# Hybrid attention block on one core: a new account of a shared port in the planner, GpSimd kept out of the feed-forwards, a new order of the mixers

## The chip, the core and the metric

The kernel runs on one core of a Trainium2 chip. Five engines take part: TensorE (PE in the profile, its weight loads PEld) multiplies matrices, VectorE (DVE) and ScalarE (ACT) work element by element, GpSimd (POOL) does the same where both operands lie in SBUF, and SyncE (SP) issues the transfers from memory. Each engine serves its own queue in order and waits on semaphores for the others. The metric is the time of one execution in microseconds of the device; lower is better.

## The reference

Two layers of a diffusion transformer block over 512 latent tokens and 256 context tokens, 1024 wide, in float32. Per layer: modulation columns from a condition vector, a norm, one projection into the inputs of three mixers (neighbourhood attention, latent attention, a gated linear recurrence), the mixers, an output projection with a residual, a second norm, and a gated feed-forward of width 2816 with a residual.

```python
for l in range(DEPTH):
    sh_m, sc_m, g_m, sh_f, sc_f, g_f = _adaln(c, ada_w[l], ada_b[l])
    u = _modulate(_rmsnorm(h, norm_mix_g[l]), sh_m, sc_m) @ w_in[l]
    ...
    o_lat = jnp.concatenate([na_o, mla_o, lru_o], axis=-1)
    h = h + g_m * (o_lat @ w_out[l])
    h = h + g_f * _swiglu(_modulate(_rmsnorm(h, norm_ffn_g[l]), sh_f, sc_f),
                          ffn_w_gate[l], ffn_w_up[l], ffn_w_down[l])
    if not last:
        ...   # the same for the context tokens hc
return h
```

The last layer gives only the latent tokens, so its feed-forward has 512 columns, the first layer's 768.

## The kernel before

Tokens lie along the free dimension, channels along the partitions. Each float32 factor is split into a high part, rounded to the matmul's format, and the low rest (`split`, made of `copy` and `sub`, lines 544 to 554); a product is three matmuls (high x high, high x low, low x high). A weight tile lands in `wst`, its parts are `whi` and `wlo`; activations in pairs are `s`, other tiles `tmp`, `lo`, `hr`; `A` and `B` are accumulator tiles; `ast` and `acc` are weights and sums of modulation columns that are worked off as a fill beside other work.

The feed-forward (`ffn`, line 1441) uses a scheme with seven half-size products in place of eight. Its operands are made first, in `operands` (line 836): norms, sums and differences of column halves, and a split of each. The weights' sums and differences (`weights`, line 884) are made from two landed tiles: these are the instructions `wst<-wst,wst`. Then come 11 pairs of hidden tiles in six groups, each group ended by a part of the down projection (`deliver`, line 1376).

No instruction is issued as it is written. Every call records an operation with its cost on each engine that may run it: `"svg"` means ScalarE, VectorE or GpSimd, `"vg"` VectorE or GpSimd. `Order.place` (line 304) then runs through a model of the machine: for each engine it takes the operation that can start first (ties by rank), lets one with several engines run where the model ends it first, and keeps in `port` when VectorE and GpSimd hold a port to SBUF that the model takes them to share. An operation that would start while the other holds it starts when that ends:

```python
if e == "g" or e == "v" and op.both:
    a, b = port["v" if e == "g" else "g"]
    if a <= st < b:
        st = b
```

`both` marks operations with no operand in the accumulators. GpSimd has a handicap of 600 in `BIAS`. Each tag (`s6`, `wst`, ...) has a number of buffers; the model keeps the times at which they come free, and `Buf.tile` asks the tile pool for one of the tag, and the pool chooses the place. In a mixer the steps are recorded in the order of `PLAN`, with a shift of rank after each `@`. Roots (the power of -0.5 in `rstd`, line 674) run on GpSimd alone.

## Time and profile before

| | |
|---|---|
| three timed runs | 1825.57, 1832.43, 1832.73 us; median 1832.43 us |
| profiled execution | 1837.95 us, span 1835.4 us |
| TensorE busy | 1720.5 us (94%) |
| VectorE busy | 1340.2 us (73%) |
| ScalarE busy | 770.2 us (42%) |
| GpSimd busy | 407.5 us (22%) |
| first mixer, about | 50 to 503 us |
| first feed-forward, about | 503 to 1090 us, its operands to 560 |
| second mixer, about | 1090 to 1455 us |
| second feed-forward, about | 1455 to 1836 us, its operands to 1500 |

A row of a profile names line, engine, operation and the tiles out<-in without buffer numbers. Most lines are helpers: L518 is every matmul, L554 every operation with two tensors, L544 and L546 the copies and casts on ScalarE and VectorE, L588 a tensor with a scalar and a tensor, L697 the root. The time of a row is the engine's busy time, which includes what the engine spends held up inside an instruction; idle time stands apart, with what ended it.

### The profile page before, as it was taken

To read this page: it belongs to the slowest core of one execution; us is meant where nothing else is said; L and a number is where in the kernel's file an instruction comes from. 1 tells how busy PE (TensorE), PEld (TensorE's weight loads), DVE (VectorE), ACT (ScalarE), POOL (GpSimd) and SP (SyncE) were. 2 spreads that over 40 slices of the span, in tenths; PEclk is the share of its full clock that TensorE was granted. 3 is DMA by queue.
4 is the path that set the end of the run, shared out by engine and by line. 5 is a ranking of instruction groups with operands and counts; after the bars stand their busy time and mean duration, and the time that the engine had idled before them with its cause. 6 is when DMAs were issued, how large, how long until landed. Compare 5 with 4: busy or idle time off the path is not lost.

```text
span 1835.4 us, 27989 instructions
## 1 busy us (share of the span) xinstructions
PE 1720.5 (94%) x10616; PEld 1472.5 (80%) x10616; DVE 1340.2 (73%) x2361; ACT 770.2 (42%) x1382; POOL 407.5 (22%) x326
## 2 busy tenths in 40 slices
PE   8989999999979999999999989998889989999998
PEld 4877665767959898989899968776678788898897
DVE  6574356766498888877879677576686797788776
ACT  5282245664153343323223233744565343343343
POOL 0142133233072121210111022213243240001010
PEclk9999899999989999999999989999999989999999
DMA  8121123233012334243434141212011123323332
GB/s 336 58 74 62 39 69 104 78 116 127 29 35 90 105 98 129 81 141 112 151 125 138 61 142 47 65 58 72 24 38 30 35 65 108 104 93 98 98 104 92
DMA packets 90998, 166.66 MB, mean 91 GB/s; under 512 B 10480, under 2 KB 53872, under 8 KB 90864
## 3 DMA queue, kind: packets, MB, share of 16 engines
q1 hardware_dynamic: 90864, 164.88, 28.1%
q8 instruction: 83, 1.36, 0.3%
q14 instruction: 51, 0.42, 0.1%
HBM read 160.65 MB, written 4.19 MB: 90 GB/s over the span
## 4 chain that ended last, share of the span: by engine, by line
PE 64%; DVE 22%; DMA 5%; issue 4%; ACT 3%; POOL 2%; SPq 0%; DVEq 0%; ACTq 0%; POOLq 0%
PE A L518 36%; PE B L518 22%; DVE wlo L554 6%; PE B L524 5%; DVE tmp L554 3%; DMA ast<-in_ada_dram 3%; DVE s L554 3%; DVE wst L554 2%; DMA wst<-in_wg_dram 1%; DVE acc L588 1%; POOL rn L697 1%; DVE s L546 1%; DVE lo L588 1%; DVE lo L554 1%; DVE hr L588 1%
## 5 line engine op out<-in xcount | busy, mean ns | idle before, releaser
L518 PE MATMUL A<-s,whi 128*128 128x256 f32 (+2 forms) x2192 | 546.9, 341 | 17.6 <-ACT s L544 5.5
L518 PE MATMUL B<-s,whi 128*128 128x384 f32 (+2 forms) x2032 | 465.9, 323 | 17.8 <-ACT hr L544 4.3
L518 PEld LDWEIGHTS A<-s,whi 128*128 128x128 f32 x2192 | 375.5, 190 | 72.2 <-ACT s L544 7.4
L544 ACT CAST whi<-wst 128x1024 fp32r<-128x1024 f32 (+2 forms) x281 | 227.0, 817 | 439.9 <-PE A L518 225.8
L518 PEld LDWEIGHTS B<-s,whi 128*128 128x128 f32 x2032 | 347.6, 193 | 32.2 <-ACT hr L544 4.6
L518 PE MATMUL A<-s,wlo 128*128 128x256 f32 (+2 forms) x1064 | 345.7, 338 | 1.2 <-DVE wlo L554 1.2
L554 DVE TENSOR_TENSOR wlo<-wst,whi 128x1024 fp32r<-128x1024 f32 (+3 forms) x303 | 319.9, 1066 | 12.1 <-ACT whi L544 8.4
L518 PE MATMUL B<-s,wlo 128*128 128x384 f32 (+2 forms) x1016 | 301.9, 320 | 0.2 <-DVE wlo L554 0.2
L518 PE MATMUL A<-lo,whi 128*128 128x512 f32 (+1 forms) x776 | 216.7, 358 | 4.7 <-DVE hr L588 1.8
L518 PEld LDWEIGHTS A<-s,wlo 128*128 128x128 f32 x1064 | 197.4, 191 | 15.8 <-DVE wlo L554 2.0
L518 PEld LDWEIGHTS B<-s,wlo 128*128 128x128 f32 x1016 | 190.6, 193 | 3.4 <-DVE wlo L554 0.5
L697 POOL TENSOR_TENSOR rn<-rn,con 128x12 f32<-128x12 f32 (+5 forms) x44 | 84.6, 1925 | 445.0 <-DVE rn L561 437.8
L518 PEld LDWEIGHTS A<-lo,whi 128*128 128x128 f32 x776 | 136.6, 188 | 31.7 <-issue 3.3
L588 DVE SCALAR_TENSOR_TENSOR hr<-A,mod,hr 128x512 f32<-128x512 f32 (+1 forms) x153 | 100.6, 659 | 60.2 <-PE A L518 60.1
L554 POOL TENSOR_TENSOR wst<-wst,wst 128x512 f32<-128x512 f32 x35 | 54.3, 1553 | 371.2 <-DVE wst L554 328.1
L518 PE MATMUL A<-lo,wlo 128*128 128x512 f32 (+1 forms) x388 | 136.2, 356 | 0.0
L518 PE MATMUL A<-s,s 128*128 128x512 f32 (+1 forms) x508 | 120.5, 354 | 14.2 <-ACT lo L533 4.5
L518 PEld LDWEIGHTS A<-s,s 128*128 128x128 f32 x508 | 81.2, 194 | 36.5 <-ACT lo L533 10.1
L546 DVE CAST whi<-wst 128x1024 fp32r<-128x1024 f32 (+3 forms) x45 | 32.7, 727 | 101.1 <-PE A L518 82.0
L588 DVE SCALAR_TENSOR_TENSOR acc<-ast,cc,acc 128x256 f32<-128x256 f32 x168 | 88.5, 527 | 19.2 <-DMA ast<-in_ada_dram 17.8
L554 POOL TENSOR_TENSOR wlo<-wst,whi 128x512 fp32r<-128x512 f32 (+3 forms) x25 | 40.9, 1637 | 262.2 <-ACT whi L544 260.9
L518 PE MATMUL B<-s,s 128*64 128x256 f32 (+2 forms) x720 | 87.5, 347 | 0.7 <-DVE sm L1411 0.5
(206 smaller groups left out, 2371.4 us busy)
## 6 DMA issues: line engine op xcount, KB each, us to landing
ast<-in_ada_dram SPq DMA_DIRECT2D x320, 128.0 KB, 2.2
wst<-in_wg_dram SPq DMA_DIRECT2D x44, 512.0 KB, 3.5
wst<-in_wu_dram SPq DMA_DIRECT2D x44, 512.0 KB, 3.5
wst<-in_wd_dram SPq DMA_DIRECT2D x80, 256.0 KB, 2.7
wst<-in_win_dram SPq DMA_DIRECT2D x32, 512.0 KB, 3.7
wst<-in_wout_dram SPq DMA_DIRECT2D x16, 512.0 KB, 3.7
hr<-in_x_dram SPq DMA_DIRECT2D x16, 384.0 KB, 3.6
s<-in_ada_dram SPq DMA_DIRECT2D x8, 768.0 KB, 11.5
```

Of the source, the lines that this page charges most:

```text
L518: od.add({"t": c}, lambda e: nc.tensor.matmul(ap(out), lhsT=ap(lhsT), rhs=ap(rhs), start=start, stop=stop, skip_group_check=more), [out], ...
L524: od.add({"t": 109.0}, lambda e: nc.tensor.transpose(ap(out), ap(in_), ap(ident)), [out], [in_, ident])
L544: nc.scalar.copy(out=ap(out), in_=ap(in_))
L546: nc.vector.tensor_copy(ap(out), ap(in_))
L554: (nc.vector if e == "v" else nc.gpsimd).tensor_tensor(out=ap(out), in0=ap(a), in1=ap(b), op=op)
L588: lambda e: nc.vector.scalar_tensor_tensor(out=ap(out), in0=ap(a), scalar=ap(s), in1=ap(b), op0=op0, op1=op1),
L697: lambda e: nc.gpsimd.tensor_tensor(out=ap(r[:, :w]), in0=ap(r[:, :w]), in1=ap(C("mhalf", 0, w)), op=ALU.pow),
```

## The change

Four edits. **The port's model:** an operation is no longer put off while the other engine holds the port. It starts, and its cost grows by the time until the other is done; in the choice between engines the same time is added. **GpSimd in the feed-forwards:** with `od.alone` set, an operation that may run on several engines loses GpSimd. It is set in `operands` and in the loop over the hidden groups. What has GpSimd as its only engine (the roots) stays there. **Buffer places:** the model keeps the number of each free buffer beside its time, hands it to the tile as `slot`, and each place is a tag of its own with one buffer; the pool chooses no more. **The mixers:** both texts of `PLAN` are new, with other orders of steps and other shifts.

```diff
@@ -57,29 +57,29 @@
 PLAN, LEAD = [], {}
 for _text in ("""
-    latent_kv @-53, lru_out 1 @-1529, lru_in 0, lru_in 1 @20, near_v 1 @990, near_q 1, lru_gates 0 @695,
...
+    lru_start @133, lru_in 0, latent_kv @1410, near_v 1 @-2446, lru_in 1 @-141, lru_out 1, lru_gates 0 @-229,
...
@@ -115,14 +115,15 @@
 
     def tile(self):
         if self.real is None:
-            self.real = self.pool.tile(list(self.shape), self.dt, tag=self.tag, name=f"{self.tag}_{self.id}",
-                                       bufs=self.bufs)
+
+            tag = self.tag if self.bufs == 1 else f"{self.tag}_{self.slot}"
+            self.real = self.pool.tile(list(self.shape), self.dt, tag=tag, name=f"{self.tag}_{self.id}", bufs=1)
         return self.real
 
 
 class Tag:
     def __init__(self, bufs):
-        self.line, self.free, self.loose = [], [0.0] * bufs, 0
+        self.line, self.free, self.loose = [], [(0.0, i) for i in range(bufs)], 0
 
 
 class Ref:
@@ -240,7 +241,7 @@
 
     def __init__(self):
         self.ops, self.bufs, self.tags = [], [], {}
-        self.shift, self.lead, self.gate = 0, 0, None
+        self.shift, self.lead, self.gate, self.alone = 0, 0, None, False
 
     def add(self, cost, emit, writes, reads, table=None, heat=1.0, middle=False, shape=0, both=False):
 
@@ -248,6 +249,8 @@
 
         op = Op()
         op.heat, op.pe, op.middle, op.shape, op.both = heat, "t" in cost, middle, shape, both
+        if self.alone and len(cost) > 1:
+            cost = {e: c for e, c in cost.items() if e != "g"}
         op.i, op.emit, op.cost, op.table = len(self.ops), emit, cost, table
         op.rank = op.i + self.shift + self.lead
         deps = {}
@@ -349,13 +352,9 @@
                                        not b.loose and len(tg.free) <= j + 1):
                             blocked = True
                             break
-                        st = max(st, tg.free[j])
+                        st = max(st, tg.free[j][0])
                     if blocked:
                         continue
-                    if e == "g" or e == "v" and op.both:
-                        a, b = port["v" if e == "g" else "g"]
-                        if a <= st < b:
-                            st = b
                     if op.table is not None and e == "s" and table not in op.table:
                         st_key = st + 1300.0
                     elif e == "t" and op.shape != shape:
@@ -371,6 +370,10 @@
 
                     op = top[1]
                     fin_here = top[3] + op.cost[e] + BIAS[e]
+                    if e == "g" or e == "v" and op.both:
+                        a, b = port["v" if e == "g" else "g"]
+                        if a <= top[3] < b:
+                            fin_here += b - top[3]
                     other = min(max(clock[x], op.ready[x]) + op.cost[x] + BIAS[x] for x in op.cost)
                     fin_key = (top[0][0] + (0.0 if fin_here <= other + 1.0 else fin_here - other), op.rank)
                     top = (fin_key, op, e, top[3])
@@ -392,7 +395,7 @@
                     tg.loose += 1
                 else:
                     tg.line.remove(b)
-                tg.free.pop(0)
+                b.slot = tg.free.pop(0)[1]
             cost = op.cost[e]
             if e == "t":
                 if op.shape != shape:
@@ -400,6 +403,10 @@
                     cost += SWITCH
                 cost = clockgate.run(st, cost, op.heat)
             if e == "g" or e == "v" and op.both:
+
+                a, b = port["v" if e == "g" else "g"]
+                if a <= st < b:
+                    cost += b - st
                 port[e] = (st, st + cost)
             if e == "s" and op.table is not None and table not in op.table:
                 table = op.table[0]
@@ -417,7 +424,7 @@
                 if not b.users and not b.dram:
                     tg = self.tags[b.tag]
                     tg.loose -= b.loose
-                    tg.free.append(b.end)
+                    tg.free.append((b.end, b.slot))
                     tg.free.sort()
             for q in op.outs:
                 q.ndep -= 1
@@ -877,8 +884,10 @@
                 tt(right(4 + j), right(4 + j), right(j), ALU.subtract)
                 put(("T4", "T3"), j, pair(), 0, xs[4 + j][:, :n])
 
+        od.alone = True
         first()
         second()
+        od.alone = False
         return ops
 
     def weights(src, i):
@@ -1528,6 +1537,7 @@
             split(two[0][:, :H], two[1][:, :H], gate.u, "s")
             return [one, two]
 
+        od.alone = True
         for h0, hn in GROUPS:
             acts = []
             for i in range(h0, h0 + hn, 2):
@@ -1543,6 +1553,7 @@
             end = h0 + hn == HT
             stats = deliver(l, h, lambda ot: load_w(wd_d[l, ot, :, h0 * P : (h0 + hn) * P], hn * P, "s"), acts, 40, n,
                             parts(n) if end and l < DEPTH - 1 else None)
+        od.alone = False
         return stats
 
     units = [0]
```

What this does to the order, at three places. First GpSimd's queue at the start of the first feed-forward, before, from the two roots on (`rn`):

```order
L697 TENSOR_TENSOR rn_5098<-rn_5098,con_82 128x3
L697 TENSOR_TENSOR rn_5105<-rn_5105,con_82 128x3
L554 TENSOR_TENSOR wst_5062<-wst_4710,wst_5062 128x512
L554 TENSOR_TENSOR s_1114_5133<-lo_5114,s_1114_5133 128x384
L548 TENSOR_SCALAR s_1116_5154<-lo_5136 128x384
L554 TENSOR_TENSOR s_1115_5150<-lo_5125,s_1115_5150 128x384
L554 TENSOR_TENSOR s_1116_5154<-lo_5136,s_1116_5154 128x384
L548 TENSOR_SCALAR s_1115_5150<-lo_5168 128x384
L554 TENSOR_TENSOR s_1115_5150<-lo_5168,s_1115_5150 128x384
L548 TENSOR_SCALAR s_1117_5194<-lo_5142 128x384
L548 TENSOR_SCALAR s_1117_5194<-lo_5158 128x384
```

The same place now:

```order
L704 TENSOR_TENSOR rn_5098<-rn_5098,con_84 128x3
L704 TENSOR_TENSOR rn_5108<-rn_5108,con_84 128x3
L555 TENSOR_SCALAR whi_10437<-wst_10361 128x1024
L561 TENSOR_TENSOR wlo_10451<-wst_10313,whi_10425 128x1024
L561 TENSOR_TENSOR wlo_10467<-wst_10417,whi_10459 128x1024
L704 TENSOR_TENSOR rn_10493<-rn_10493,con_84 128x4
L704 TENSOR_TENSOR rn_10532<-rn_10532,con_84 128x2
```

After the two roots nothing of the feed-forward follows; the next row (`whi_10437`) belongs to the second layer's first weights, and the roots of that layer's norm stand behind a cast and two subtractions, as they do before.

VectorE's queue at the same start, before, in the last third of the operands:

```order
L554 TENSOR_TENSOR s_1124_5276<-tmp_5256,s_1124_5276 128x768
L554 TENSOR_TENSOR wlo_5309<-wst_5102,whi_5296 128x1024
L554 TENSOR_TENSOR s_1126_5306<-tmp_5281,s_1126_5306 128x768
L554 TENSOR_TENSOR lo_5168<-lo_5168,lo_5125 128x384
L546 COPY tmp_5337<-B_5200 128x384
L554 TENSOR_TENSOR wlo_5345<-wst_4770,whi_5322 128x1024
L554 TENSOR_TENSOR s_1128_5333<-lo_5158,s_1128_5333 128x768
L554 TENSOR_TENSOR wlo_5366<-wst_5062,whi_5351 128x1024
L554 TENSOR_TENSOR s_1130_5360<-hr_5178,s_1130_5360 128x768
L554 TENSOR_TENSOR wlo_5387<-wst_5254,whi_5376 128x1024
L554 TENSOR_TENSOR wst_5373<-wst_5373,wst_5254 128x512
```

And now:

```order
L561 TENSOR_TENSOR lo_5143<-lo_5143,lo_5110 128x384
L561 TENSOR_TENSOR lo_5154<-lo_5154,lo_5120 128x384
L561 TENSOR_TENSOR wlo_5320<-wst_5102,whi_5308 128x1024
L561 TENSOR_TENSOR lo_5171<-lo_5171,lo_5127 128x384
L561 TENSOR_TENSOR hr_5183<-hr_5183,lo_5137 128x384
L561 TENSOR_TENSOR s_1127_5317<-lo_5143,s_1127_5317 128x768
L561 TENSOR_TENSOR wlo_5350<-wst_4771,whi_5338 128x1024
L561 TENSOR_TENSOR wlo_5361<-wst_5059,whi_5346 128x1024
L561 TENSOR_TENSOR s_1128_5325<-lo_5154,s_1128_5325 128x768
L561 TENSOR_TENSOR s_1129_5356<-lo_5171,s_1129_5356 128x768
L561 TENSOR_TENSOR s_1130_5364<-hr_5183,s_1130_5364 128x768
```

The `lo`, `hr` and `s` instructions that were GpSimd's stand between the weights' subtractions: of eleven rows four are differences, four low halves and three the weights' work, where one was a difference, four were low halves, one a copy and five the weights' work.

TensorE's queue in the second mixer, at a step that transposes copies of a value tile (`pvt`), before, from the last matmuls of a job on:

```order
L518 MATMUL B_12878<-s_2472_12830,s_2252_11889 64x256
L518 MATMUL B_12878<-s_2481_12862,s_2252_11889 64x256
L524 MATMUL B_12966<-ident_65,pvt_12942 128x128 x2
L524 MATMUL B_12970<-ident_65,hr_11936 128x128 x2
L518 MATMUL A_12974<-s_2122_11239,s_2383_12563 128x512 x3
L518 MATMUL A_12974<-s_2122_11239,s_2383_12563 128x256 x3
L518 MATMUL A_12990<-s_2122_11239,s_2383_12563 128x512
```

And now, up to the transposes of the copy made at about the same place:

```order
L531 MATMUL B_12932<-ident_65,pvt_12097 128x128 x2
L525 MATMUL B_12929<-s_2473_12861,s_2247_11972 64x256
L525 MATMUL A_12942<-s_2115_11161,s_2383_12573 128x512
L531 MATMUL B_12948<-ident_65,hr_11340 128x128 x2
L525 MATMUL A_12942<-s_2115_11161,s_2383_12573 128x512 x2
L525 MATMUL A_12942<-s_2115_11161,s_2383_12573 128x256
L531 MATMUL B_12955<-ident_65,lo_12927 128x128
L531 MATMUL B_12957<-ident_65,pvt_12940 128x128 x2
```

Between the first transposes of a `pvt` and the next there are now matmuls of a score tile `A` and a transpose of another step; before, the transposes of `pvt_12942` and of the tile `hr_11936` follow the job's last matmul at once.

## Rows read from the trace of the kernel before

**Rows 1.** The page's head.
```profile
span 1835.4 us, 27989 instructions
```

**Rows 2.** By stage: length, busy (instructions) of PE, PEld, DVE, ACT, POOL, clock, DMA.
```profile
50.00:503.00 453.00, 430.29 (x2804) 334.65 (x2804) 266.85 (x534) 202.52 (x407) 125.28 (x97) 0.99 0.24 75
503.00:560.00 57.00, 40.55 (x198) 35.44 (x197) 52.18 (x75) 30.97 (x55) 36.84 (x27) 0.85 0.12 37
560.00:1090.00 530.00, 511.28 (x2915) 479.30 (x2914) 427.84 (x736) 173.19 (x276) 80.97 (x59) 1.00 0.37 115
1090.00:1455.00 365.00, 333.90 (x2108) 270.83 (x2108) 255.73 (x442) 183.63 (x340) 107.13 (x85) 0.95 0.16 50
1455.00:1500.00 45.00, 36.31 (x215) 33.40 (x214) 42.15 (x67) 24.58 (x48) 28.60 (x30) 0.77 0.15 48
1500.00:1836.00 336.00, 325.54 (x2170) 295.63 (x2168) 259.50 (x400) 130.54 (x215) 26.25 (x22) 1.00 0.31 98
```

**Rows 3.** TensorE's waits, 560 to 1090 us: who for whom, sum, times, longest.
```profile
PE B L518 <- DVE acc L588: 5.5, 5, 1.7
PE A L518 <- ACT s L544: 3.7, 4, 1.3
PE B L518 <- DVE tmp L554: 2.8, 3, 1.4
PE A L518 <- DVE tmp L554: 2.1, 4, 0.7
```

**Rows 4.** Timeline of VectorE, 538 to 555 us: start, duration, operation.
```profile
...
544.02 2.39 DVE L554 TENSOR_TENSOR wlo<-wst,whi 128x1024 fp32r<-128x1024 f32 x1
...
548.86 2.29 DVE L554 TENSOR_TENSOR wlo<-wst,whi 128x1024 fp32r<-128x1024 f32 x1
...
553.00 1.21 DVE L554 TENSOR_TENSOR wlo<-wst,whi 128x1024 fp32r<-128x1024 f32 x1
```

**Rows 5.** Timeline of GpSimd, the same stretch.
```profile
...
543.17 4.94 POOL L554 TENSOR_TENSOR s<-lo,s 128x768 fp32r<-128x768 f32 x2
548.08 1.98 POOL L554 TENSOR_TENSOR wst<-wst 128x512 f32<-128x512 f32 x1
550.14 2.12 POOL L554 TENSOR_TENSOR wst<-wst,wst 128x512 f32<-128x512 f32 x1
```

**Rows 6.** Groups of VectorE, 503 to 1090 us: busy us, mean ns, idle before.
```profile
L554 DVE TENSOR_TENSOR wlo<-wst,whi 128x1024 fp32r<-128x1024 f32 x64 | 89.1, 1408 | 0.8 <-ACT whi L544 0.5
L588 DVE SCALAR_TENSOR_TENSOR acc<-ast,cc,acc 128x256 f32<-128x256 f32 x168 | 88.5, 527 | 19.2 <-DMA ast<-in_ada_dram 17.8
...
L554 DVE TENSOR_TENSOR wst<-wst,wst 128x512 f32<-128x512 f32 x40 | 34.3, 861 | 0.1
```

**Rows 7.** Groups of VectorE, 803 to 835 us, in which GpSimd runs nothing.
```profile
L588 DVE SCALAR_TENSOR_TENSOR acc<-ast,cc,acc 128x256 f32<-128x256 f32 x8 | 3.8, 479 | 0.1
L554 DVE TENSOR_TENSOR wlo<-wst,whi 128x512 fp32r<-128x512 f32 x5 | 3.4, 682 | 0.0
...
L554 DVE TENSOR_TENSOR wlo<-wst,whi 128x1024 fp32r<-128x1024 f32 x2 | 2.5, 1225 | 0.0
L554 DVE TENSOR_TENSOR wst<-wst,wst 128x512 f32<-128x512 f32 x3 | 2.0, 685 | 0.0
L554 DVE TENSOR_TENSOR lo<-tmp,lo 128x768 fp32r<-128x768 f32 x1 | 0.9, 946 | 0.0
...
L554 DVE TENSOR_TENSOR tmp<-tmp,tmp 128x384 f32<-128x384 f32 x1 | 0.5, 547 | 0.0
```

**Rows 8.** Groups of GpSimd, 503 to 1090 us.
```profile
L554 POOL TENSOR_TENSOR wst<-wst,wst 128x512 f32<-128x512 f32 x23 | 38.5, 1676 | 231.8 <-DVE wst L554 200.3 <-DVE wlo L554 16.5 <-DMA ast<-in_ada_dram 14.8
L554 POOL TENSOR_TENSOR wlo<-wst,whi 128x512 fp32r<-128x512 f32 x12 | 17.6, 1466 | 83.5 <-ACT whi L544 83.5
```

**Rows 9.** TensorE's waits, 1090 to 1455 us.
```profile
PE B L524 <- POOL rn L697: 6.8, 2, 6.2
PE B L524 <- DVE pvt L546: 5.2, 4, 3.1
```

More of the change, by code (lines that the diff above doesn't have):

```diff
@@ new lines @@
+    latent_query 3 @56, latent_job 0 0 @523, near_bias 0, latent_put 1 @497, latent_job 1 2 @465,
+    latent_query 4 @-1072, latent_job 1 0 @442, latent_query 5 @-990, latent_job 1 1, near_job 0 1 @38,
+    latent_put 2 @61, out_part 1 @64, near_job 0 0 @-1, near_ctx 0 @-2037, latent_job 2 0 @-6, near_prep 2 @460,
+    near_bias 2 @-49, out_part 3 @-1893, latent_job 2 2 @-44, out_part 0 @-98, latent_job 2 1 @-896,
+    near_prep 1 @-11, near_job 2 0 @-53, near_job 2 1 @1, out_part 2 @109, near_ctx 1 @-50, near_bias 1 @821,
@@ new lines @@
+    near_ctx 2 @-7, near_job 1 0 @-20, out_part 4 @-974, near_job 1 1 @87, out_part 6 @-5, out_part 5 @361,
+    out_part 7
+""", """
+    latent_kv @-2, lru_in 0 @-45, lru_in 1 @110, lru_gates 0 @72, near_k 2 @-239, near_k 0, latent_k 0 @-2500,
+    lru_out 1 @462, lru_gates 1 @218, near_v 0 @2202, latent_rope @507, lru_out 0 @-158, latent_keys @-283,
+    latent_put 0, latent_q @806, latent_k 1 @-10, near_q 0 @-744, near_k 1 @-113, lru_start @-305, lru_scan 0 @768,
+    near_q 1, latent_query 1, near_q 2, latent_query 0 @-6, latent_k 2 @26, latent_v, near_v 2 @-305, near_v 1 @217,
+    near_prep 1 @-38, lru_scan 1 @56, latent_query 2 @1619, latent_job 0 0 @-131, latent_job 0 1 @1455,
+    latent_put 1 @14, latent_query 3 @82, latent_job 1 0 @191, latent_query 4 @38, latent_query 5 @68,
+    latent_job 1 1, latent_put 2, near_bias 1 @1199, latent_job 2 1 @2500, near_job 1 1 @-477, out_part 1,
+    near_job 1 0 @-700, near_prep 0 @-587, latent_job 2 0 @27, near_prep 2 @55, near_bias 0 @-103,
+    near_job 0 0 @2382, near_job 0 1, near_bias 2 @1121, out_part 0 @196, near_job 2 1 @-284, out_part 3 @21,
+    near_job 2 0 @-28, out_part 4 @1524, out_part 5 @301, out_part 7, out_part 6 @-990, out_part 2 @403
```

25 lines of the change are left out of this document (4 added, 21 removed).

## Prediction

> **What bounds the kernel now.** I read the head of the page first, then the busy times by stage, then who waits for whom on TensorE in the stages that stand out, and last single instructions where two engines meet. The profiled execution has a span of 1835.4 us [rows 1] and took 1837.95 us in all; the three timed runs have their median at 1832.43 us, 5.5 us below it. I make the sum against 1837.95 and take the 5.5 us off at the end.
>
> The table by stage [rows 2] has two stretches for each layer besides its mixer: the start of a feed-forward, in which its operands are made (503 to 560 and 1455 to 1500), and its body (560 to 1090 and 1500 to 1836). TensorE is the bound almost everywhere, and its idle time says what can be had at all: 453 - 430.3 = 22.7 us in the first mixer, 365 - 333.9 = 31.1 us in the second; 57 - 40.6 = 16.4 us and 45 - 36.3 = 8.7 us in the two starts; 530 - 511.3 = 18.7 us and 336 - 325.5 = 10.5 us in the bodies. That is 108 us; the first 50 us of the program hold the rest. In the starts VectorE is the engine that others wait for: 52.2 of 57 us and 42.2 of 45 us busy, TensorE's granted clock down to 0.85 and 0.77 on average. In the bodies VectorE is 81% and 77% busy, and where TensorE waits in the first one, it waits mostly for VectorE: 5.5, 2.8 and 2.1 us are the largest such sums, beside 3.7 us for ScalarE [rows 3].
>
> What GpSimd does in these stretches is seen from single instructions. Between 538.64 and 554.14 us VectorE never idles, yet the same subtraction of a 128x1024 tile takes 2.39 and 2.29 us and then 1.21 us [rows 4]. The first two lie beside GpSimd instructions with two tiles in SBUF; the last one begins at 553.00, after GpSimd's last one ended at 550.14 + 2.12 = 552.26 [rows 5]. So two engines at work here largely take turns.
>
> **The change, part by part.**
>
> *GpSimd out of the feed-forwards.* In the order, GpSimd's instructions between the roots ahead of the first feed-forward and the second mixer go from 84 to 5: a cast and two subtractions of the next mixer's weights and the two roots of its norm stay. In the second feed-forward they go from 49 to 1. VectorE gets 61 and 43 instructions more, ScalarE 21 and 6.
>
> First the start of the first one. In the 15.5 us from 538.64 VectorE runs nine instructions. At the durations of a stretch in which GpSimd is idle [rows 7] they come to 4 x 1.23 + 3 x 0.95 + 2 x 0.55 = 8.9 us. The six GpSimd instructions beside them, four of which stand in [rows 5], are two of 384 columns, two of 768 and two of 512: on VectorE 2 x 0.55 + 2 x 0.95 + 2 x 0.69 = 4.4 us. In one queue that is 13.3 us for 15.5, a gain of 2.2 us. In the rest of the stretch GpSimd's small casts go to ScalarE, which has room (31.0 of 57 us busy [rows 2]); I add nothing for it. The second start has tiles two thirds as wide and less GpSimd time (28.6 against 36.8 us): I take 1 us. Both ends: the two stretches' whole idle time on TensorE, 25 us, as a gain; as a loss, that VectorE takes the moved work and none of its long durations shrink. The moved additions and subtractions of the first start are some 11.5 us at the durations of rows 7, those of the second about 10; VectorE has 4.8 and 2.9 us left there, so 14 us are lost. I take -3 us, near the stretch that I could work out.
>
> Then the bodies. Taken together with the starts, three kinds of VectorE instruction show what the shared access costs: (1408 - 1225) x 64 = 11.7 us, (527 - 479) x 168 = 8.1 us and (861 - 685) x 40 = 7.0 us, 26.8 us in all [rows 6, 7]; kinds that I do not list add to it. Against it stand the moved ones: 24 + 12 of the two kinds of 128x512 in [rows 8], some three more of that size, 39 x 0.685 = 26.7 us, and about 22 others at up to 0.95 us, some 14 us: 41 us. So VectorE's total stays about where it is. What changes is when a result comes: a sum of two weight halves takes 0.69 us in place of 1.68, a low half 0.68 in place of 1.47 [rows 7, 8]. 23 x 0.99 + 12 x 0.78 = 32 us of delay go out of the chain that feeds the casts and, behind them, TensorE. Little of it is on the path: TensorE waits 18.7 us in all, and what it waits longest for is the accumulator of the modulation columns, whose instructions are among those slowed (527 for 479 ns). The three sums for VectorE in rows 3 are 10.4 us; I take a half of them, 5 us, and 2 of the second body's 10.5 us, where GpSimd has a third of the first body's time. Ends: -20 us (most of 18.7 and a bit of 10.5), and +10 us, if the fills' accumulators come later because VectorE now does GpSimd's part of them as well: what is queued behind a late accumulator on TensorE is the whole feed-forward, since a queue is served in order. I take -7 us.
>
> *The port's model and the mixers' new order.* Both change only who comes when. GpSimd keeps its share there (111 to 115 instructions in the first mixer with the program's head, 85 to 86 in the second), so its turns with VectorE stay, and no stage gets work or loses it. What can go are waits such as the 6.8 us for two roots and the 5.2 us for four copies ahead of transposes in the second mixer [rows 9]. The longest of each has a fate in the order: the root that TensorE waits 6.2 us for stands in the order behind the same three GpSimd instructions as before (a cast and two subtractions of 128x1024), so that wait stays; the copy that cost 3.1 us now has TensorE work of another kind between it and its transposes. Of the mixers' 53.8 us idle I take a tenth, -5 us. Ends: -25 us, about half of it; +20 us, if the new places suit the model and not the chip: twelve waits like the copy's 3.1 us less what went would do.
>
> *Buffer places set by the order.* Taken alone this leaves each engine's rows as they are, and only which earlier tile a few instructions wait for differs (288 of some 3,150 tiles get another predecessor, about as many a later one as an earlier one). Zero, with the waits for buffers hidden by TensorE's queue; the ends are a few us to either side, within those above.
>
> Sum: -3 - 7 - 5 = -15 us, 1837.95 - 15 = 1823 in a profiled execution, and 5.5 less as a median of runs: **1817 us**, 0.8% faster.
>
> A rule speaks against the change. The Trainium skill, "Perfetto Trace Analysis", section "Optimizing Scalar/DVE Operations", says that where DVE is saturated, handing work to Scalar or even GPSIMD may make sense, and adds that between GPSIMD and DVE it might not help since they share a read port. By the first half of it the starts, where VectorE is the saturated engine, would lose by taking work back; by the second half they would not. Rows 4 and 5 side with the second half here; the first half is what the slower rival below rests on.
>
> **The rivals.**
>
> *Slower: the starts become VectorE's.* One mechanism: GpSimd did some 21 us of VectorE's work in the two starts beside it, and taking turns was only part of it. For it speaks that VectorE is over 90% busy there and that its chain ends in TensorE's first products; against it that rows 4 show nearly every instruction stretched. It decides if the stretching gives back less than 21 - 7.7 = 14 us. If it gives nothing, +14 us and no gain in the bodies: 1832 + 14 = 1846 us. Chance 0.18, in which I count a mixer order that suits the chip less.
>
> *No change.* TensorE streams at its rate in the bodies, the delays that go were covered by its queue, and the mixers trade one wait for another; for it speaks that each wait in rows 3 and 9 is a few us, against it that a stretch like that of rows 4 has nothing to hide it. Gain 0 to 8 us, 1828 us. Chance 0.21.
>
> *Much faster: the mixers close up.* The new order takes out half of their 53.8 us of idle time, -25, with -10 from the feed-forwards: 1797 us. For it: a model that charges the port to the instruction that meets it is closer to rows 4; against it: the longest single wait of the second mixer stays. Chance 0.11.
>
> **How the numbers follow.** Forecast 0.50, slower 0.18, no change 0.21, much faster 0.11. I call 0.5% (9 us) what a measurement tells from no change. Of the forecast's case, -6 to -28 us, four fifths lie beyond 9 us: 0.40, and with the much faster case 0.51 plus a little of the others: faster 0.54, same 0.27, slower 0.19. The forecast's own range is 1804 to 1826 us. The range for 8 in 10 reaches into the cases at both sides: 1796 to 1843 us.
>
> **What would show it.** GpSimd's busy time falls by about 160 us to some 250 us, while VectorE's stays within 20 us of 1340. The subtraction of 128x1024 in the feed-forwards has a mean near 1.23 us in place of 1.41, the accumulation near 0.48. The first start gets shorter by 2 us or more and ends with TensorE's clock up no later. The 6.2 us wait for a root at the second mixer's start is still there. I am wrong if VectorE's busy time grows by the whole 64 us that it takes over, if the starts get longer, or if the mixers' lengths (453 and 365 us) move by more than 10 us either way.

## The result and the profile after

The changed kernel takes **1777.99 us** (median of four runs, 1776.80 to 1778.68) against 1831.5 us of the kernel before beside it: 0.9713 of its time, 95% interval 0.9691 to 0.9736. The forecast of 1817 us had the direction; the gain is 53.5 us, not 15, and the time lies below the range of 1796 to 1843 us.

The page's head of the changed kernel, to be read beside [rows 1] (before: GpSimd 407.5 us, VectorE 1340.2 us in 2361 instructions):
```profile
span 1776.7 us, 27829 instructions
PE 1698.7 (96%) x10616; PEld 1458.1 (82%) x10616; DVE 1308.9 (74%) x2452; ACT 783.5 (44%) x1413; POOL 248.6 (14%) x204
```
VectorE runs 91 instructions more in 31 us less.

For comparing stages I cut both traces at the same instructions: the first that makes a feed-forward's operands, the first that takes a product out of PSUM, the first of the next norm. "Start" is where a feed-forward's operands are made, "body" the rest of it. Before, first mixer to second body:
```profile
27.70:513.00 485.30, 458.11 (x2976) 354.20 (x2975) 296.43 (x605) 217.58 (x432) 127.65 (x100) 0.99 0.26 83
513.00:557.60 44.60, 30.15 (x125) 26.54 (x126) 42.53 (x55) 25.33 (x47) 32.79 (x24) 0.82 0.11 36
557.60:1096.40 538.80, 514.79 (x2933) 482.41 (x2931) 436.25 (x747) 176.37 (x281) 87.10 (x61) 0.99 0.37 114
1096.40:1456.90 360.50, 333.57 (x2107) 270.44 (x2107) 251.09 (x436) 182.63 (x338) 103.85 (x85) 0.96 0.15 49
1456.90:1487.10 30.20, 22.74 (x122) 20.27 (x121) 30.15 (x43) 17.75 (x36) 26.12 (x28) 0.74 0.17 53
1487.10:1832.50 345.40, 338.34 (x2257) 308.43 (x2257) 270.10 (x420) 137.11 (x226) 27.55 (x23) 0.99 0.31 96
```
And the changed kernel (columns of [rows 2]):
```profile
27.60:503.20 475.60, 455.62 (x2974) 353.31 (x2975) 294.21 (x600) 219.52 (x430) 131.38 (x105) 0.99 0.26 85
503.20:539.00 35.80, 28.48 (x115) 23.27 (x115) 35.76 (x68) 26.91 (x51) 0.00 (x0) 0.78 0.13 43
539.00:1059.10 520.10, 509.37 (x2946) 481.44 (x2947) 425.32 (x796) 184.68 (x297) 8.93 (x4) 0.99 0.38 120
1059.10:1413.80 354.70, 330.30 (x2107) 266.84 (x2106) 248.71 (x430) 181.88 (x343) 105.25 (x87) 0.98 0.15 48
1413.80:1443.80 30.00, 25.71 (x146) 22.57 (x146) 30.00 (x65) 21.72 (x45) 0.60 (x1) 0.77 0.16 53
1443.80:1773.80 330.00, 326.16 (x2232) 300.39 (x2232) 261.50 (x440) 135.23 (x224) 0.00 (x0) 0.99 0.31 100
```
The feed-forwards give 43 us (8.8 and 18.7 us in the first one's start and body, 0.2 and 15.4 in the second's), the mixers 15.5 us (9.7 and 5.8). The two profiled executions are 59.3 us apart (1837.95 and 1778.68), 6 more than the medians; most of that excess lies in the second body (next section). In the bodies VectorE has 49 and 20 instructions more and is busy 10.9 and 8.6 us less.

VectorE's groups from 503.2 to 1059.1 us, beside [rows 6]:
```profile
L595 DVE SCALAR_TENSOR_TENSOR acc<-ast,cc,acc 128x256 f32<-128x256 f32 x168 | 80.7, 482 | 19.7 <-DMA ast<-in_ada_dram 17.7 <-ACT acc L582 0.4
L561 DVE TENSOR_TENSOR wlo<-wst,whi 128x1024 fp32r<-128x1024 f32 x65 | 78.3, 1222 | 1.3 <-PE A L525 0.4 <-ACT whi L551 0.4
L561 DVE TENSOR_TENSOR wst<-wst,wst 128x512 f32<-128x512 f32 x63 | 42.0, 686 | 0.1
```
1408, 527 and 861 ns are now 1222, 482 and 686, within 3 ns the undisturbed durations of [rows 7]. On TensorE, 539 to 1059.1 us, beside [rows 3]: the wait for accumulators is 1.2 us in place of 5.5, and the largest sum belongs to the next norm, at the stage's end.
```profile
PE B L525 <- DVE tmp L561: 4.7, 3, 4.2
PE B L531 <- POOL rn L704: 3.3, 1, 3.3
PE B L525 <- DVE acc L595: 1.2, 2, 0.8
```

### The profile page after: what moved, and what is told of

Same layout as the page of the kernel before. It is cut to its first block, busy times and chain, and to the rows that moved or that the text cites. A ratio compares the mean times of both kernels' runs of the same rounds, so it can differ in the third digit from the quotient of the medians.

```text
span 1776.7 us, 27829 instructions
## 1 busy us (share of the span) xinstructions
PE 1698.7 (96%) x10616; PEld 1458.1 (82%) x10616; DVE 1308.9 (74%) x2452; ACT 783.5 (44%) x1413; POOL 248.6 (14%) x204
## 4 chain that ended last, share of the span: by engine, by line
PE 79%; DVE 9%; DMA 2%; ACT 2%; issue 1%; POOL 1%; SPq 0%; ACTq 0%; DVEq 0%; POOLq 0%
PE A L525 43%; PE B L525 31%; PE B L531 5%; DMA ast<-in_ada_dram 2%; DVE s L561 2%; DVE wlo L561 1%; DVE tmp L561 1%; DVE lo L595 1%; DVE s L553 1%; POOL rn L704 0%; ACT lo L540 0%; DVE acc L595 0%; DVE sm L614 0%; DVE wst L561 0%; DVE hr L595 0%
## 5 line engine op out<-in xcount | busy, mean ns | idle before, releaser
L525 PE MATMUL A<-s,whi 128*128 128x256 f32 (+2 forms) x2192 | 540.7, 338 | 10.6 <-DVE whi L553 2.0
L525 PE MATMUL B<-s,whi 128*128 128x384 f32 (+2 forms) x2032 | 456.7, 319 | 11.0 <-DVE tmp L561 3.7
L551 ACT CAST whi<-wst 128x1024 fp32r<-128x1024 f32 (+3 forms) x289 | 235.8, 827 | 415.0 <-PE A L525 228.0
L525 PEld LDWEIGHTS B<-s,whi 128*128 128x128 f32 x2032 | 341.4, 191 | 25.6 <-DVE s L561 6.7
L561 DVE TENSOR_TENSOR wlo<-wst,whi 128x1024 fp32r<-128x1024 f32 (+4 forms) x322 | 311.2, 976 | 14.0 <-ACT whi L551 9.6
L525 PE MATMUL A<-s,s 128*128 128x256 f32 (+1 forms) x508 | 119.2, 353 | 15.3 <-ACT lo L540 4.8
L595 DVE SCALAR_TENSOR_TENSOR acc<-ast,cc,acc 128x256 f32<-128x256 f32 x168 | 80.7, 482 | 19.7 <-DMA ast<-in_ada_dram 17.7
L561 DVE TENSOR_TENSOR wst<-wst,wst 128x512 f32<-128x512 f32 x132 | 87.8, 690 | 0.5
L555 POOL TENSOR_SCALAR whi<-wst 128x1024 fp32r<-128x1024 f32 x6 | 7.9, 1319 | 572.9 <-PE B L525 548.4
L551 ACT COPY s<-B 128x384 f32<-128x384 f32 (+2 forms) x143 | 63.8, 476 | 39.7 <-PE B L531 35.0
```

The costliest lines, as they stand in the source:

```text
L525: od.add({"t": c}, lambda e: nc.tensor.matmul(ap(out), lhsT=ap(lhsT), rhs=ap(rhs), start=start, stop=stop, skip_group_check=more), [out], ...
L551: nc.scalar.copy(out=ap(out), in_=ap(in_))
L555: nc.gpsimd.tensor_scalar(out=ap(out), in0=ap(in_), scalar1=1.0, scalar2=1.0, op0=ALU.mult, op1=ALU.mult)
L561: (nc.vector if e == "v" else nc.gpsimd).tensor_tensor(out=ap(out), in0=ap(a), in1=ap(b), op=op)
L595: lambda e: nc.vector.scalar_tensor_tensor(out=ap(out), in0=ap(a), scalar=ap(s), in1=ap(b), op0=op0, op1=op1),
```

## The experiments

Stage lengths below are between the same marks, in us, of one profiled execution (the edits follow); times are medians, ratios are to the kernel before run beside it, with 95% intervals. Stages in order: first mixer, start, body; second mixer, start, body.

| kernel | time, ratio | M1 | S1 | B1 | M2 | S2 | B2 |
|---|---|---|---|---|---|---|---|
| before | 1831.5 | 485 | 44.5 | 539 | 360.5 | 30.1 | 345 |
| changed | 1778.0, 0.9713 | 476 | 35.8 | 520 | 354.7 | 30.0 | 330 |
| a_alone | 1795.7, 0.9808 (0.9788-0.9828) | 480 | 36.5 | 519 | 355.5 | 30.7 | 334 |
| a_port | 1865.4, 1.0184 (1.0166-1.0203) | 506 | 43.2 | 540 | 373.9 | 30.0 | 341 |
| slots | 1832.6, 0.9995 (0.9980-1.0011) | 487 | 43.2 | 540 | 360.4 | 30.1 | 341 |
| a_plan2 | 1833.2, 1.0000 (0.9979-1.0022) | 488 | 40.6 | 538 | 364.6 | 30.2 | 340 |
| u_alone | 1819.8, 0.9924 (0.9901-0.9946) | 479 | 44.9 | 541 | 352.5 | 32.6 | 338 |
| u_plan | 1828.6, 0.9974 (0.9958-0.9990) | 507 | 36.8 | 517 | 370.7 | 30.7 | 332 |
| u_port | 1798.7, 0.9814 (0.9786-0.9842) | 486 | 36.8 | 518 | 362.2 | 30.4 | 331 |
| o_body | 1806.1, 0.9850 (0.9821-0.9878) | 486 | 45.2 | 520 | 357.8 | 33.5 | 333 |
| o_operands | 1827.5, 0.9970 (0.9950-0.9989) | 487 | 34.8 | 544 | 356.5 | 24.9 | 347 |
| t_late | 1780.5, 0.9705 (0.9678-0.9732) | 479 | 36.8 | 518 | 352.7 | 31.1 | 331 |
| t_beside | 1801.1, 0.9811 (0.9783-0.9840) | 477 | 35.8 | 522 | 355.0 | 31.4 | 346 |
| t_beside4 | 1825.2, 0.9960 (0.9945-0.9975) | 478 | 36.5 | 533 | 354.6 | 31.4 | 360 |
| w_on | 1800.0, 0.9815 (0.9790-0.9840) | 477 | 35.0 | 531 | 357.2 | 30.1 | 336 |
| f_on | 1796.4, 0.9806 (0.9787-0.9825) | 477 | 35.8 | 527 | 357.3 | 30.7 | 335 |
| x_all | 1884.6, 1.0272 (1.0244-1.0300) | 569 | 35.8 | 515 | 369.3 | 30.1 | 333 |
| b_bound | 1788.6, 0.9754 (0.9730-0.9778) | 479 | 35.8 | 515 | 363.5 | 30.7 | 331 |
| b_loads | 1800.5, 0.9826 (0.9801-0.9850) | 479 | 35.8 | 515 | 379.8 | 29.8 | 330 |

Before's B2 is 345 us in this one profile and 340 to 341 in three others that leave the body as it was, so some 5 of the 15.4 us belong to that execution. Stage lengths of single executions can be off by that much: a_alone's profile (1787.45 us) is its fastest run, 8 us under its median.

**One part done alone.** a_alone: the kernel before with
```diff
+        od.alone = True
         first()
         second()
+        od.alone = False
...
+        od.alone = True
         for h0, hn in GROUPS:
...
+        od.alone = False
```


> The kernel before with one part of the change: GpSimd takes no work in the feed-forwards (neither in the start nor in the body); table of the order, port model and buffer places as before. Theory A (most of the 54 us is GpSimd leaving the feed-forwards: VectorE's instructions no longer stretched beside it, and results earlier): 35 to 45 us faster than before, 1787 to 1797 us, with the two feed-forwards 30 us or more shorter and the mixers within 4 us. Theory B (most is the new table and port model, which fit each other): 5 to 15 us faster, 1817 to 1827 us. Prediction's slower rival (the starts become VectorE's): over 1832 us.

It is 38 us faster, as theory A has it, and the feed-forwards are 38 us shorter. The mixers are 5 us shorter each, where theory A allowed 4; that is in the one fast execution.

a_port: the kernel before with the new port model's lines only.
```diff
-                    if e == "g" or e == "v" and op.both:
-                        a, b = port["v" if e == "g" else "g"]
-                        if a <= st < b:
-                            st = b
...
+                a, b = port["v" if e == "g" else "g"]
+                if a <= st < b:
+                    cost += b - st
```


> The kernel before with one part of the change: only the new port model (an instruction that meets the other engine's starts at once and is charged the rest of its turn); GpSimd keeps its work in the feed-forwards. Theory A: within 9 us of before, 1823 to 1841 us. Theory B: 15 to 25 us faster, 1807 to 1817 us, mixers and feed-forwards alike.

Both theories missed: it is 32 us slower, all of it in the mixers (20.6 and 13.4 us).

slots: the kernel before with
```diff
+            tag = self.tag if self.bufs == 1 else f"{self.tag}_{self.slot}"
```
and the free list that carries the places.

> The kernel before with one part of the change: only the buffer places set by the order. Each engine's queue is that of before, row for row. Theories A and B alike: within 4 us of before, 1828 to 1836 us, no stage moved by more than 2 us. A theory that the places take out buffer waits by themselves would want 1820 us or less.

Nothing, as expected; only B2 moved by more than 2 us, by the 5 named above.

a_plan2: that, and the new table.
```diff
-    latent_kv @-53, lru_out 1 @-1529, lru_in 0, lru_in 1 @20, ...
+    lru_start @133, lru_in 0, latent_kv @1410, near_v 1 @-2446, ...
```


> The kernel before with the new table of the order and the buffer places set by the order (the new table is not tried without them), old port model, GpSimd at work in the feed-forwards as before. Theory A: 8 to 16 us faster, 1816 to 1824 us, all of it in the mixers. Theory B (table and port model belong together): 0 to 10 us slower than before alone, since the table suits another model. A theory that the new table is what shortens the feed-forwards too: 40 us faster.

No change, which is nearest to theory B; the table under the old model is worth nothing.

**One part undone.** u_alone: the changed kernel without `od.alone = True`, at both places.
```diff
-        od.alone = True
```


> The changed kernel with one part undone: GpSimd works in the feed-forwards again, as before; new table, new port model and new places stay. Theory A (GpSimd leaving the feed-forwards is worth 35 to 45 us whatever else is there): 30 to 45 us slower than the changed kernel, 1808 to 1823 us, with the feed-forwards 28 us or more longer and the mixers as changed (within 5 us). Theory B (with the table that belongs to it the new port model finds good turns for GpSimd): 1785 to 1800 us.

Theory A: 42 us slower than the changed kernel, the mixers as short as there.

u_plan: the changed kernel with the old table (the diff of a_plan2 reversed).
```diff
-    lru_start @133, lru_in 0, latent_kv @1410, ...
+    latent_kv @-53, lru_out 1 @-1529, lru_in 0, ...
```


> The changed kernel with one part undone: the table of the order of before, with the new port model, without GpSimd in the feed-forwards, new places. The model alone cost 20 and 13 us in the two mixers (run with only the model changed: 505.9 and 373.9 us for 485.3 and 360.5). Theory C (table and model belong together; each is worth something only with the other): mixers near 505 and 374 us, feed-forwards as changed, so 1815 to 1830 us. Theory D (the loss of the model came through the feed-forwards' queues): 1785 to 1800 us.

Theory C: the mixers lose what they lost in a_port, the feed-forwards keep their gain.

u_port: the changed kernel with the old port model.
```diff
-                if a <= st < b:
-                    cost += b - st
...
+                        if a <= st < b:
+                            st = b
```


> The changed kernel with one part undone: the port model of before, with the new table, without GpSimd in the feed-forwards, new places. With GpSimd in the feed-forwards the table under the old model was as fast as before (mixers 488.2 and 364.6 us). Theory C: mixers near those, feed-forwards near the changed ones: 1790 to 1800 us. A theory that the table alone brings the mixers' 15 us once the feed-forwards are clean: 1775 to 1783 us.

Theory C again. With these, table and model are tried in all four pairs, each with and without GpSimd in the feed-forwards. GpSimd's leaving is worth 37.8, 36.8, 34.5 and 41.8 us (old table and model; new model; new table; both new; slots shows that the places, which differ among these, are worth nothing by themselves). The pair is worth 13.5 us with GpSimd there (1833.3 to 1819.8) and 17.7 without (1795.7 to 1778.0); the model without the table costs 32 us, the table without the model brings nothing.

**Which place.** o_body and o_operands: the kernel before with one of the two places.
```diff
+        od.alone = True
         for h0, hn in GROUPS:
```


> The kernel before with GpSimd taken out of the feed-forwards' bodies only; in the starts, where the operands are made, it works as before. Taking it out of both took 19.8 us (first) and 11.1 us (second) off the bodies and 8 us off the first start. Theory A1 (each place pays for itself): bodies as there, the first start near 44.5 us, 1800 to 1808 us. Theory A2 (the bodies gain because the starts hand over earlier): bodies shorter by at most 10 us together, 1818 to 1828 us.

1806.1 us: the bodies pay for themselves.
```diff
+        od.alone = True
         first()
         second()
+        od.alone = False
```


> The kernel before with GpSimd taken out of the starts only, where the feed-forwards' operands are made; in the bodies it works as before. The prediction gave this 3 us, by one stretch of 15.5 us. With both places taken out the first start was 8 us shorter and the second no shorter (run on the table of before); with the bodies alone 1806 us was measured against 1796 for both. If the starts pay for themselves: 1822 to 1828 us, the first start near 36.5 us. If they pay only together with the bodies (their work ends in the same queues): 1829 to 1836 us.

6 us, at the edge of what "the starts pay for themselves" wanted: both starts are shorter (9.7 and 5.2 us), but the bodies are longer by 5 and 2 in the one profile.

**Late or long?** What GpSimd did to a body is of two kinds: its results came later, and VectorE's instructions beside it took longer. t_late brings back some of the first alone. GpSimd multiplies four columns of each sum by one, and the sum's users wait for it; the model is told of 1 us and leaves this instruction out of the port:
```diff
             tt(sums[:, :Q], two[:, :Q], two[:, Q:], ALU.add)
+            later_by(sums[:, :4])
```


> The changed kernel plus a delay without two-tile work on GpSimd: in the feed-forwards' bodies each sum of two weight halves (44 of them) goes on to its users only after GpSimd has multiplied four of its columns by one (a 128x4 instruction); the order is told of it with 1 us. So each sum comes about a microsecond later, as it did when GpSimd made it (1.68 us for 0.69), and VectorE is next to undisturbed. Theory E (contention): within 8 us of the changed kernel, 1770 to 1786 us. Theory F (latency): 15 to 30 us longer, 1793 to 1808 us.

The same time as the changed kernel. This is not the same lateness as before. What is late here is the sum (`wst<-wst`), and GpSimd had made only one of those in the two bodies of before; it had made 30 of the differences (`wst<-wst,wst`), and of a weight's three differences two wait for the sum, directly or through another. Low halves, accumulators and activations were not delayed by themselves. But the trace of before speaks against them too: in its bodies the profile shows no idle time of TensorE or VectorE that a GpSimd instruction ended, except TensorE's 6.2 us for the norm's root; ScalarE has 2.9 and 0.8 us.

t_beside brings back the second alone:
```diff
-            tt(sums[:, Q:], sums[:, :Q], one[:, :Q], ALU.subtract)
+            beside(sums[:, Q:], sums[:, :Q], one[:, :Q], ALU.subtract, 2)
...
+            for x in [b, a] * reads:
+                nc.gpsimd.tensor_tensor(out=junk[0][:, :], in0=ap(x[:, :184]), in1=ap(x[:, 184:368]), op=ALU.add)
```


> The changed kernel, each engine's queue as it is there, plus work on GpSimd that nobody waits for: in the feed-forwards' bodies, beside each difference of a weight's half sums (44 of them), four additions of 128x184 from tiles in SBUF into a tile that nobody reads. GpSimd gets some 90 us of busy time back in the bodies, VectorE keeps all of its work, and no result comes from GpSimd. Theory E (contention: VectorE's instructions get long beside GpSimd's, and that is what the bodies gained): both bodies together 15 to 30 us longer, 1793 to 1808 us. Theory F (latency: what the bodies gained is that the results no longer come from a slow engine): within 6 us of the changed kernel, 1773 to 1784 us.

It costs 23 us, 15.8 of them in the second body and 2.3 in the first. (A tile that GpSimd reads comes free later: transfers wait for this work four times in the whole trace, 2.2 us in all, and ScalarE twice, 2.2 us.) One such place in the second body, first GpSimd, then VectorE, then TensorE (start, duration):
```profile
1526.30 2.62 POOL L601 TENSOR_TENSOR junk<-wst 128x184 f32<-128x184 f32 x3 [7.57 <-DVE wst L561]
```
```profile
1525.46 0.69 DVE L561 TENSOR_TENSOR wst<-wst 128x512 f32<-128x512 f32 x1
1526.06 0.42 DVE L561 TENSOR_TENSOR s<-tmp,s 128x256 fp32r<-128x256 f32 x1
1526.40 1.08 DVE L597 TENSOR_TENSOR wst<-wst,wst 128x512 f32<-128x512 f32 x1
1527.40 1.07 DVE L561 TENSOR_TENSOR wst<-wst,wst 128x512 f32<-128x512 f32 x1
1528.40 2.74 DVE L561 TENSOR_TENSOR wlo<-wst,whi 128x1024 fp32r<-128x1024 f32 x2
```
```profile
1527.83 1.37 PE L525 MATMUL B<-s,whi 128*128 128x256 f32 x10
1530.06 0.74 PE L525 MATMUL B<-s,wlo 128*128 128x256 f32 x4 [0.86 <-DVE wlo L561]
```
Two differences of 128x512 take 1.08 and 1.07 us for 0.69, the low halves behind them in VectorE's queue come later, and TensorE stands 0.86 us for one of them. By kind, over the second body, t_beside and then the changed kernel:
```profile
PE A L525 <- DVE tmp L561: 4.1, 7, 0.7
PE B L525 <- DVE tmp L561: 3.9, 2, 3.2
PE B L525 <- DVE wlo L561: 3.4, 4, 0.9
```
```profile
PE B L525 <- DVE tmp L561: 3.2, 1, 3.2
PE A L525 <- ACT lo L551: 0.9, 1, 0.9
PE A L525 <- DVE tmp L561: 0.2, 1, 0.2
```
The second body of t_beside in the table by stage:
```profile
1449.60:1795.40 345.80, 332.82 (x2232) 302.09 (x2232) 279.71 (x440) 135.54 (x224) 72.26 (x79) 1.00 0.32 96
```
It runs the 2232 matmuls and the 440 VectorE instructions of the changed kernel's second body. The 15.8 us stand as 9.1 us of idle time on TensorE (13.0 for 3.8) and as 6.7 us of busy time (332.8 for 326.2). How a stall can be busy time: a matmul's row is longer than its step; ten of 128x256, each a row of some 0.28 us, fill 1.37 us above, so (1.37 - 0.28) / 9 = 0.12 us from one to the next. So a stall under 0.28 - 0.12 = 0.16 us between two of them leaves no idle time.

**Which instructions.** t_beside4 doubles that work (`4` for `2`).
```diff
-            beside(sums[:, Q:], sums[:, :Q], one[:, :Q], ALU.subtract, 2)
+            beside(sums[:, Q:], sums[:, :Q], one[:, :Q], ALU.subtract, 4)
```


> As the run with work on GpSimd that nobody waits for, with twice the amount: eight additions of 128x184 beside each of the 44 differences of half sums instead of four. The four cost 23 us (first body 2.3, second 15.8). If what counts is how much of VectorE's time is stretched: some 20 us more, 1815 to 1830 us, and the first body at 530 us or more. If the first body has room beside the weights' work and only the second's is on the path: first body 522 to 528 us, second 350 to 362 us, 1805 to 1820 us.

24 us more, and now the first body pays too (13.2 us over the changed kernel; the second 30.3). w_on gives GpSimd back the work on the gate's and up's weights that is recorded in `prepare`, f_on all else. The edit of w_on; f_on has the two values the other way round and drops the `True` ahead of the loop:
```diff
             keep, od.shift = od.shift, -LOAD_EARLY
+            od.alone = False
...
             od.shift = keep
+            od.alone = True
```


> The changed kernel with GpSimd back in the feed-forwards' bodies for the weights alone (sums of halves, low halves, casts); the accumulators of the modulation, the activations and the starts stay without it. Theory G (the first body's 20 us come from the weights' instructions too, by their number): first body 533 to 541 us, second 337 to 342 us, 1795 to 1808 us. Theory H (the first body's time goes where GpSimd meets the accumulators that TensorE waits for): first body 518 to 526 us, second 333 to 342 us, 1780 to 1793 us.

> The changed kernel with GpSimd back in the feed-forwards' bodies for everything but the weights: some 18 instructions on the modulation's accumulators, the activations and their low halves. Theory G (weights): within 6 us of the changed kernel, 1773 to 1784 us. Theory H (accumulators and activations, on which TensorE waits at once): first body 530 to 541 us, second within 4 us of 330, 1788 to 1802 us.

f_on is not "everything but the weights". The down projection's weights are split outside `prepare`, so GpSimd makes low halves of weights again, 12 of 128x512 in the first body and 5 in the second. In w_on it makes none of them, only sums and differences. In f_on, 540 to 1060 us:
```profile
L561 POOL TENSOR_TENSOR wlo<-wst,whi 128x512 fp32r<-128x512 f32 x12 | 18.3, 1525 | 76.0 <-ACT whi L551 72.6 <-DVE s L561 3.4
```
Neither theory alone, then, and the two runs do not part the weights from the rest: the sums and differences cost the bodies 11.3 and 6.3 us, the low halves with the accumulators and activations 7.1 and 5.1. Together that is 18.4 and 11.4; GpSimd cost 20.4 and 7.5 in u_alone.

The runs can be set side by side by how much VectorE was stretched. For each kind of VectorE instruction (same tiles, same shape) that the changed kernel's body has too, I take its mean duration less its mean there, times its count, and add up the kinds (us):

| | before | u_alone | w_on | f_on | t_beside | t_beside4 |
|---|---|---|---|---|---|---|
| first body: stretched by | 37.6 | 41.2 | 17.9 | 16.5 | 12.4 | 24.0 |
| first body: longer by | 18.7 | 20.4 | 11.3 | 7.1 | 2.3 | 13.2 |
| second body: stretched by | 17.8 | 15.6 | 8.1 | 5.8 | 18.4 | 35.9 |
| second body: longer by | 15.4 | 7.5 | 6.3 | 5.1 | 15.8 | 30.3 |

More stretching goes with a longer body, whether GpSimd's results are used (the first four) or not. The second body pays most of it, the first about half, and a fifth in t_beside.

**Going further.** x_all takes GpSimd out of the mixers as well.
```diff
-        self.shift, self.lead, self.gate, self.alone = 0, 0, None, False
+        self.shift, self.lead, self.gate, self.alone = 0, 0, None, True
```


> The changed kernel with GpSimd out of the mixers as well: whatever another engine can do is done there, only roots and what has no other engine stay. In the changed kernel VectorE's instructions are still some 34 us longer in the mixers than without GpSimd beside them, and GpSimd is busy there for some 230 us, of which VectorE would take about a half. If the feed-forwards' rule holds for the mixers: mixers 5 to 20 us shorter, 1758 to 1773 us. If VectorE, at 65 to 77% there, needs the second engine, or the table fits only the order that it was made for: mixers 5 to 25 us longer, 1783 to 1803 us.

107 us slower than the changed kernel. Its first mixer:
```profile
27.60:596.00 568.40, 494.89 (x2973) 369.80 (x2973) 305.32 (x664) 235.50 (x452) 41.71 (x20) 0.91 0.23 71
```
VectorE is busy for 54% of it, which speaks against too much work on VectorE; which part of the new order loses the time was not pursued.

b_bound keeps GpSimd from the second mixer's first four weight tiles, b_loads from all its weights (`loads[0]` counts them; b_loads has 99 for the 4).
```diff
-        split(hi, lo, st, engs)
+        keep, od.alone = od.alone, od.alone or 0 < loads[0] <= 4
+        split(hi, lo, st, engs)
+        od.alone = keep
```


> The changed kernel with GpSimd kept from the first four weight tiles of the second mixer (a cast and two subtractions of 128x1024 stood on GpSimd just ahead of the norm's roots). If they hold the second mixer's start: the wait of 4.2 us for the norm's squares and the 3.3 us for the root shrink to 5 us or less together, 3 to 7 us faster than the changed kernel, 1771 to 1775 us. If VectorE, which takes the subtractions, is as late with the norm's sums: 1776 to 1781 us.

> As the run before, with GpSimd kept from every weight tile of the second mixer (casts and low halves); activations, copies and roots stay on it. If contention costs the mixer as it costs a body (half of VectorE's lengthening there, 17.6 us, from the weights): 5 to 12 us faster than the changed kernel, 1766 to 1773 us. If the table of the order fits only the placement that it was made with: mixer longer by 5 to 20 us, 1783 to 1798 us.

Both missed. The place itself does gain: in the changed kernel VectorE's sums for the norm are held up beside GpSimd's subtraction, and the root follows (VectorE and GpSimd):
```profile
1052.83 3.42 POOL L561 TENSOR_TENSOR wlo<-wst,whi 128x1024 fp32r<-128x1024 f32 x1 [0.80 <-ACT whi L551]
1053.97 2.57 DVE L561 TENSOR_TENSOR tmp<-tmp,tmp 128x256 f32<-128x256 f32 x1
1056.68 1.19 POOL L704 TENSOR_TENSOR rn<-rn,con 128x4 f32<-128x4 f32 x1 [0.44 <-DVE rn L568]
```
Without it the first body ends 5.4 us sooner (515 for 520), and the second mixer takes 8.8 and 25.1 us longer. In b_bound 7.7 us go in its first 50: the same 244 matmuls need 51.8 us for 44.1, first b_bound, then the changed kernel:
```profile
1056.70:1108.50 51.80, 46.94 (x244) 38.67 (x244) 37.80 (x62) 18.56 (x27) 9.95 (x11) 0.89 0.17 52
```
```profile
1059.10:1103.20 44.10, 43.50 (x244) 36.30 (x243) 34.84 (x57) 18.71 (x28) 9.86 (x11) 0.93 0.12 37
```
No version beat the changed kernel.

## Why the prediction was wrong in size

*Starts, -3 us.* In the traces -8.8 and -0.2; 6 us alone (o_operands). The first start was worked out from one stretch of 15.5 us and taken for the whole, which gained four times that. VectorE fills 35.76 of its 35.8 us now, in 68 instructions for 55. The rule weighed there, the Trainium skill's "Perfetto Trace Analysis", section "Optimizing Scalar/DVE Operations", comes out by its second half in these starts: between GpSimd and VectorE handing work over did not help, although VectorE was busy for 42.5 of 44.6 us and 30.15 of 30.2 us; taking the work back gave 6 us.

*Bodies, -7 us.* The step that failed. The prediction set 26.8 us of stretching against 41 us of moved work ("So VectorE's total stays about where it is"), and then looked for the gain in 32 us of late results ("Little of it is on the path"), of which TensorE's named waits let it keep 7. The runs point the other way. A microsecond on each of the 44 sums cost nothing (t_late). Stretched instructions cost nearly all they were stretched by in the second body (t_beside: VectorE's busy time 18.2 us more, the body 15.8 more) and less in the first until the dose is doubled. Why the first body gives less at the low dose stays open, and so does what share of its gain is lateness of a kind that t_late did not try. The stretching was also counted short: the three kinds are 23.6 of 37.6 us in the first body, and the second body's 17.8 us had no term. VectorE's total fell by 31 us where 20 either way were allowed. The gain, -18.7 and -15.4 us in these traces (some 5 of the second are that execution's), -19.8 and -11.1 in a_alone, is together four to five times the -7.

*The cap.* That TensorE's "idle time says what can be had at all" was wrong as well, though the sum of 108 us was not reached. In the second body TensorE was idle for 345.4 - 338.3 = 7.1 us before, and the body got 15.4 us shorter (some 10 without that execution's 5). Each feed-forward taken whole runs as many matmuls as before (3058 and 3061, 2379 and 2378); of 43.1 us TensorE's idle time gave 26.8 and its busy time 16.3, and t_beside shows how a stall gets into busy time.

*Mixers, -5 us.* -9.7 and -5.8; the pair of table and model is worth 13.5 to 17.7 us. I said that both change only who comes when, which holds, and took a tenth of the idle time without a reason for the tenth. That they are worth something only together was not seen; a_port alone loses 32 us, more than the +20 that the prediction gave to places that "suit the model and not the chip". Which waits make up that loss, or the gain, was not pursued.

*Places, 0.* Right (slots).

*The signs.* The subtraction's 1.23 and the accumulation's 0.48 us came as said, GpSimd fell by 159 us, and the clock was low in the first start for no longer (means of 0.82 over 44.6 us and 0.78 over 35.8 us: some 16 us at the lower level in both). The 6.2 us wait for a root, said to stay, became one of 3.3 us behind one of 4.2 us for the norm's squares; before, those two were 6.2 and 1.4, so together they did stay. The mixers moved by 9.7 and 5.8 us, just inside the 10 that would have been a sign of being wrong.

*The rivals.* The starts as VectorE's: no; in every run without GpSimd in the starts the two together are shorter than before. No change: no. Much faster by the mixers: its 1797 us came nearest, with the parts exchanged, the feed-forwards giving 43 and the mixers 15.

## What to carry to other kernels

Where two engines take turns at memory, price a hand-over by what it does to the durations of both queues, over all kinds of instructions, and read those against undisturbed rows of the same trace. Here results that came a microsecond late were covered; instructions that took longer in a full queue were paid for, mostly by half or more. TensorE's idle time was no cap on the gain, since its rows overlap and swallow short stalls: compare lengths of stages with equal counts of matmuls. The planner's model and the table that goes with it were one part here, and had to be changed and tried together.

## What the runs showed of the hardware

GpSimd instructions of 128x4 left VectorE alone: beside 18 of them, 0.66 us each, between 560 and 1050 us of t_late, VectorE's differences of 128x512 have a mean of 683 ns, against 686 in the changed kernel. Instructions with two tiles in SBUF lengthen both engines' work: VectorE's differences took 861 ns before [rows 6], and of GpSimd's 35 in the trace of before 21 took 1.26 to 1.30 us, the rest up to 2.68. VectorE's instructions with an operand in the accumulators kept their length: `hr<-A,mod,hr` of 128x512 has a mean of 749 ns in the first body both before and after. First t_late, then w_on, where GpSimd has differences and a few sums again:
```profile
L594 POOL TENSOR_SCALAR wst<-wst 128x4 f32<-128x4 f32 x18 | 11.8, 657 | 435.8 <-DVE wst L561 235.1 <-ACT acc L582 84.0 <-ACT tmp L540 49.2
...
L561 DVE TENSOR_TENSOR wst<-wst,wst 128x512 f32<-128x512 f32 x55 | 37.3, 683 | 0.4
```
```profile
L561 POOL TENSOR_TENSOR wst<-wst,wst 128x512 f32<-128x512 f32 x21 | 42.6, 2032 | 409.9 <-DVE wst L561 288.1 <-DMA ast<-in_ada_dram 57.4 <-ACT acc L582 42.6
L561 POOL TENSOR_TENSOR wst<-wst 128x512 f32<-128x512 f32 x2 | 8.4, 4199 | 46.2 <-PE A L525 31.8 <-DMA ast<-in_ada_dram 14.5
```
A difference that VectorE makes in 0.69 us takes GpSimd 2.03 us here on average, and the two sums 4.2 us.
